# Strassen parts for the first twelve blocks of the opening group, weight sums and gating on GpSimd

## The chip, the cores and the metric

The kernel runs on one core of a Trainium2 chip. The metric is the device time of one execution in microseconds (us); lower is better. The engines are TensorE (PE in the profile; PEld are its weight loads), VectorE (DVE), ScalarE (ACT), GpSimd (POOL) and SyncE (SP), which issues most of the DMAs in the order of its queue. An engine works through its own instructions in order, and an instruction that waits holds up all that stand behind it on that engine.

## The reference

One layer of a hybrid encoder over 2048 prompt tokens and 64 sample tokens, 1024 channels, float32. Cut to what matters:

```python
h = rmsnorm(x, g1) * (1 + sc1) + sh1
u, q, k, v, o, gates = split(h @ w_in)
mix = concat([pool_mixer(u), mlstm(q, k, v, gates) * sigmoid(o)]) @ w_out
x = x + gt1 * mix                                   # attention half
h2 = rmsnorm(x, g2) * (1 + sc2) + sh2
up = h2 @ w_up                                      # 1024 -> 2 * 2816
a, g = split(b_conv + causal_conv3(up, w_conv))
x = x + gt2 * ((silu(g) * a) @ w_down)              # feed-forward half
y = rmsnorm(x, g_final)
```

## The kernel before, in words

**Precision.** Each operand of a product is split into a high and a low part (`wt[:, 0]` and `wt[:, 1]` for weights): ACT copies the value into the reduced float format, DVE subtracts to get the rest. A product then takes three passes of TensorE (`PASSES`). Weights come as a stream of units of up to 512 columns (`stream`, `issue`, `work_on`): a DMA on SP, the copy on ACT (L428), the subtraction on DVE (L431). The stream runs a few units ahead of TensorE (`pump`).

**Attention half.** Four groups of 512 tokens (the last with the 64 sample tokens as well, 576). Each group projects, runs four mLSTM heads and four pooling rows (`poolmix`, whose small copies of `u` are on POOL), and then the output projection `outproj`: eight rows of 128 output channels, each with two weight units (`w_out`, then `wo_in`), two banks of PSUM, an `x` row loaded by SP, an add on DVE (L267 by `now`), a store to `x2d` and a square on ACT that is added into `ssum`. Side work is written as generators in the lists `bg`, and the matmul loops advance them a step at a time (`tick`). One of them, `up_sums`, starts with group 1 and makes the sums of `w_up` that the feed-forward half needs: for each of 22 feature blocks and two halves it loads a tile `w4` (four buffers), does four operations on 128x256, and stores the result to `wsum`, 44 steps in all. Its instructions are pinned in program order.

At the end of the last group, after the first two output rows, `outproj` calls `leave`. It empties all these generators (`drain`), closes the storage of the attention half, opens that of the feed-forward half in its place, and starts `norm_sums`, which makes the operand sums of the opening feed-forward group: ACT issues loads of `h2d`, ACT and DVE form the tiles `hx` (L809, L795, L791).

**Feed-forward half.** Three groups of 704 tokens (`fgroups`). The up projection uses a Strassen scheme for each of the 22 feature blocks (`Pair`): seven products of operand sums (`B11`, `B21`, `T1` to `T4`, `B22`) with weights or weight sums, each 12 matmuls of 352 columns (L1616). Then the convolution (L1589, L1594), silu on ACT (L1812), gating on DVE (`Pair.gate`, L1817 and L1820), and the split of the gated rows. The blocks of a group are cut into parts (`PARTS`). A part of four blocks takes its down projection by the same scheme (`quad_down`, 168 matmuls of 352 columns, L2084), with weight sums `dsum` of `w_quad`; any other part takes the plain one (`down`, L2230: per block 8 rows x 3 passes x two column ranges of 448 and 256, so 48 matmuls). In the opening group the parts are of 6, 6, 4 and 6 blocks, only the third is a Strassen part, and `quad_sums` makes all of `dsum` on DVE as side work in that group (L1676 to L1682). In the other two groups the parts are 4, 4, 4, 4 and 6.

In the opening group three of the four weight sums of a block (`KEPT`) are split and written to `wsplit`, from which the other groups load them whole.

Of the kernel before, what the change touches and what calls it, by code (L numbers as in the profile page):

```python
# [9 lines left out]
F32 = mybir.dt.float32  # L10
F32R = mybir.dt.float32r
AF = mybir.ActivationFunctionType
ALU = mybir.AluOpType
# [53 lines left out]
def tile_layer(ctx: ExitStack, tc: tile.TileContext, xT, vecs, cst, rst, w_mod, w_ada, w_qkou, w_v, w_pool,  # L67
# [273 lines left out]

    def sum_unit(g, f, i):
# [16 lines left out]
    for g in range(NFG):  # L359
        held = None  # L360
        late = []
        for (f0, f1_) in PARTS[g]:
# [21 lines left out]
            late = []  # L384
    pend = []
# [38 lines left out]
    def work_on(u, upto):  # L424
# [5 lines left out]
        if u.state == 1 and upto > 1:  # L430
            dve.tensor_tensor(out=u.w[:, 1, :u.n], in0=u.raw[:, :u.n], in1=u.w[:, 0, :u.n].bitcast(F32), op=ALU.subtract)  # L431
            u.state = 2
# [434 lines left out]
    if True:  # L867
# [6 lines left out]
        def up_sums():  # L874

            def load(f, c):
                w = a1.tile([P, 4, 256], F32, tag="w4", name="w4", bufs=4)
                for i in range(2):
# [3 lines left out]
            todo = [(f, c) for f in range(NF) for c in (0, 256)]  # L882
# [3 lines left out]
            def store():  # L886
                if made:
                    f, c, w = made.pop()
                    pin(nc.sync.dma_start(out=wsum[f, :, :, c:c + 256], in_=w))
            yield  # L890
            yield
            for i, (f, c) in enumerate(todo):
# [9 lines left out]
                pin(dve.tensor_tensor(out=a0, in0=g1, in1=a0, op=ALU.subtract))  # L902
                pin(dve.tensor_tensor(out=a1_, in0=a1_, in1=a0, op=ALU.subtract))
# [762 lines left out]
    def quad_sums(ds):  # L1666

        for d in ds:
            for c in (0, 256):
                t = f2.tile([P, 2, FT], F32R, tag="av", name="qs", bufs=AVB)  # L1670
                w = t.bitcast(F32).rearrange("p a t -> p (a t)")[:, :1024].rearrange("p (i c) -> p i c", i=4)
                nc.sync.dma_start(out=w, in_=w_quad[d, :, :, c:c + 256])
                for _ in range(7):
                    yield
                a11, a12, a21, a22 = (w[:, i] for i in range(4))
                dve.tensor_tensor(out=a22, in0=a21, in1=a22, op=ALU.add)  # L1676
                yield
                dve.tensor_tensor(out=a21, in0=a11, in1=a21, op=ALU.subtract)
                yield
                dve.tensor_tensor(out=a11, in0=a22, in1=a11, op=ALU.subtract)  # L1680
                yield
                dve.tensor_tensor(out=a12, in0=a12, in1=a11, op=ALU.subtract)  # L1682
                yield
                yield
                nc.sync.dma_start(out=dsum[d, :, :, c:c + 256], in_=w)
                yield
                yield

# [20 lines left out]
    class Pair:  # L1709


        ended = False
# [7 lines left out]
        def products(self, old):  # L1720
# [45 lines left out]
            product(b3, Bo, "T3", False)  # L1766
            rest((older, Pair.step_7))
# [46 lines left out]
        def gate(self):  # L1814
            E = EX - 2 if self.o.last else FT
            if self.quad is None:
                dve.tensor_tensor(out=self.tg[:, :E], in0=self.ta[:, :E], in1=self.tg[:, :E], op=ALU.mult)  # L1817
                return
            for (a, b, s) in self.o.segs:
                dve.tensor_tensor(out=self.tg[:, a:b], in0=self.ta[:, a + 2 * s:b + 2 * s], in1=self.tg[:, a + 2 * s:b + 2 * s],  # L1820
# [342 lines left out]
    for o in fgroups:  # L2163
        Bo = B[o.g]
        held = None
        for pi, part in enumerate(PARTS[o.g]):
# [6 lines left out]
            if quad is not None and o.g == 0:  # L2173
                drain(0)
# [216 lines left out]
```

## Time and profile before

| | |
|---|---|
| median of three runs | 2168.68 us (2167.97 to 2169.99) |
| span of the profiled execution | 2165.8 us; no time of its own is listed beside it |
| busy: PE, PEld | 2143.9, 2038.3 us |
| busy: DVE, ACT, POOL | 1649.8, 1105.2, 265.3 us |
| HBM | 412.56 MB read, 125.98 MB written |

The profile is one execution. Its rows group instructions by line, engine and tiles: busy time, mean length in ns, and the idle time of the engine before them with what ended it. A row of a timeline begins with the start and the length in us, counted from the start of the span. A row of windows has the busy time of each engine in that stretch, with the number of instructions. Line numbers of the change below differ from those of before by some: L431 becomes L437, L898 to L903 become L908 to L913, L2084 becomes L2077, L2230 becomes L2216.

### The profile page before, as it was taken

To read this page: it belongs to the slowest core of one execution; us is meant where nothing else is said; L and a number is where in the kernel's file an instruction comes from. 1 tells how busy PE (TensorE), PEld (TensorE's weight loads), DVE (VectorE), ACT (ScalarE), POOL (GpSimd) and SP (SyncE) were. 2 spreads that over 40 slices of the span, in tenths; PEclk is the share of its full clock that TensorE was granted. 3 is DMA by queue.
4 is the path that set the end of the run, shared out by engine and by line. 5 is a ranking of instruction groups with operands and counts; after the bars stand their busy time and mean duration, and the time that the engine had idled before them with its cause. 6 is when DMAs were issued, how large, how long until landed. Compare 5 with 4: busy or idle time off the path is not lost.

```text
span 2165.8 us, 38050 instructions
## 1 busy us (share of the span) xinstructions
PE 2143.9 (99%) x13529; PEld 2038.3 (94%) x13529; DVE 1649.8 (76%) x3060; ACT 1105.2 (51%) x2193; POOL 265.3 (12%) x475
## 2 busy tenths in 40 slices
PE   8999999999999999999999999999999999999998
PEld 7888888888899999999999999999999999999998
DVE  5777679677675778788688768988877597887874
ACT  4554335234333557465556445655655365565554
POOL 0010000001000301010001220100101321111112
PEclk9999999999999999999999999999999999999999
DMA  8987997897799689797768976665668675555542
GB/s 320 331 304 225 325 311 249 292 325 259 247 294 296 207 273 317 241 343 248 229 219 305 360 282 207 228 225 202 219 234 276 221 251 190 171 175 188 172 159 76
DMA packets 297063, 541.09 MB, mean 250 GB/s; under 512 B 25728, under 2 KB 113280, under 8 KB 296872
## 3 DMA queue, kind: packets, MB, share of 16 engines
q1 hardware_dynamic: 286280, 513.44, 70.3%
q10 hardware_dynamic: 10592, 25.20, 3.0%
q8 instruction: 107, 1.75, 0.3%
q14 instruction: 84, 0.69, 0.1%
HBM read 412.56 MB, written 125.98 MB: 249 GB/s over the span
## 4 chain that ended last, share of the span: by engine, by line
PE 89%; DVE 4%; DMA 3%; issue 1%; ACT 1%; SPq 0%; POOL 0%; POOLq 0%; DVEq 0%; ACTq 0%
PE mm L1616 37%; PE mm L495 23%; PE mm L2230 11%; PE mm L2084 10%; PE mm L1155 3%; DVE wt L431 1%; PE m L1345 1%; PE m L1365 1%; PE m L1367 1%; PE m L1330 1%; DMA wt<-dsum 0%; PE mm L1091 0%; DMA qs<-w_quad 0%; DVE tg L1594 0%; DMA raw<-w_up 0%
## 5 line engine op out<-in xcount | busy, mean ns | idle before, releaser
L1616 PE MATMUL mm<-hx,wt 128*128 128x352 f32 x5544 | 886.1, 321 | 2.5 <-DVE wt L431 2.2
L1616 PEld LDWEIGHTS mm<-hx,wt 128*128 128x128 f32 x5544 | 878.3, 188 | 4.9 <-DVE wt L431 4.2
L495 PE MATMUL mm<-hl,wt 128*128 128x512 f32 (+2 forms) x1920 | 385.4, 356 | 0.0
L431 DVE TENSOR_TENSOR wt<-raw,wt 128x512 fp32r<-128x512 f32 (+1 forms) x460 | 310.8, 681 | 79.1 <-ACT wt L428 77.7
L428 ACT ACTIVATE wt<-raw 128x512 fp32r<-128x512 f32 (+1 forms) x460 | 274.7, 604 | 168.0 <-PE mm L495 53.2
L495 PEld LDWEIGHTS mm<-hl,wt 128*128 128x128 f32 x1920 | 314.7, 188 | 47.4 <-issue 4.4
L2084 PE MATMUL mm<-av,wt 128*128 128x352 f32 x1512 | 248.0, 323 | 1.7 <-DVE x L2053 0.7
L2084 PEld LDWEIGHTS mm<-av,wt 128*128 128x128 f32 x1512 | 242.3, 188 | 4.8 <-DVE ea L1625 2.8
L2230 PE MATMUL mm<-av,wt 128*128 128x448 f32 (+1 forms) x1440 | 231.4, 322 | 0.0
L2053 DVE SCALAR_TENSOR_TENSOR x<-mm,MOD,x 128x352 f32<-128x352 f32 (+3 forms) x368 | 171.9, 507 | 77.8 <-PE mm L2230 62.0
L2230 PEld LDWEIGHTS mm<-av,wt 128*128 128x128 f32 x1440 | 220.8, 188 | 9.7
L1664 ACT ACTIVATE mm<-mm 128x352 f32<-128x352 f32 x204 | 91.4, 448 | 238.9 <-PE mm L1616 175.1
L495 PE MATMUL mm<-mx,wt 128*128 128x512 f32 (+1 forms) x960 | 182.6, 352 | 0.0
L495 PEld LDWEIGHTS mm<-mx,wt 128*128 128x128 f32 x960 | 159.3, 188 | 22.5
L1594 DVE SCALAR_TENSOR_TENSOR ta<-ea,V,ta 128x704 f32<-128x704 f32 (+1 forms) x132 | 125.7, 953 | 60.4 <-ACT ta L1589 56.3
L1594 DVE SCALAR_TENSOR_TENSOR tg<-eg,V,tg 128x704 f32<-128x704 f32 (+1 forms) x132 | 125.7, 952 | 49.8 <-ACT tg L1589 47.2
L431 DVE TENSOR_TENSOR wt<-wt 128x512 fp32r<-128x512 f32 x204 | 138.7, 685 | 10.9 <-ACT wt L428 10.7
L428 ACT ACTIVATE wt<-wt 128x512 fp32r<-128x512 f32 x204 | 123.8, 622 | 25.9 <-DMA wt<-wsum 24.7
L1572 POOL COPY ea<-UC 128x2 f32<-128x2 f32 x66 | 35.0, 530 | 529.1 <-DVE ta L1594 418.4
L1812 ACT ACTIVATE tg<-tg 128x704 f32<-128x704 f32 (+1 forms) x66 | 52.5, 796 | 71.3 <-DVE tg L1594 71.3
L1155 PE MATMUL mm<-wt,hl 128*128 128x256 f32 (+1 forms) x576 | 71.2, 284 | 0.0
L1155 PEld LDWEIGHTS mm<-wt,hl 128*128 128x128 f32 x576 | 70.3, 189 | 0.8 <-issue 0.6
(305 smaller groups left out, 2222.7 us busy)
## 6 DMA issues: line engine op xcount, KB each, us to landing
wt<-wsplit SPq DMA_DIRECT2D x132, 512.0 KB, 4.2
raw<-w_up SPq DMA_DIRECT2D x198, 256.0 KB, 4.1
wt<-hl_kept SPq DMA_DIRECT2D x96, 512.0 KB, 5.9
wt<-wsum SPq DMA_DIRECT2D x132, 256.0 KB, 4.9
wsplit<-wt SPq DMA_DIRECT2D x66, 512.0 KB, 5.3
w<-w_up SPq DMA_DIRECT2D x88, 256.0 KB, 4.7
wsum<-w SPq DMA_DIRECT2D x44, 512.0 KB, 5.3
Bd<-fscr ACTq DMA_DIRECT2D x56, 352.0 KB, 3.4
```

The costliest lines, as they stand in the source:

```text
L428: act.activation(u.w[:, 0, :u.n], u.raw[:, :u.n], AF.Copy)
L431: dve.tensor_tensor(out=u.w[:, 1, :u.n], in0=u.raw[:, :u.n], in1=u.w[:, 0, :u.n].bitcast(F32), op=ALU.subtract)
L495: pe.matmul(ps[bi][:, :hi - lo], U[:, a, k % 4 * P:(k % 4 + 1) * P], mv[k][:, b, lo:hi], start=(at == 0 and pi == 0), stop=(k == order[-1] ...
L1155: pe.matmul(ps[ti][:n, :cols], h[4 * kh + k4][:, b, lo:lo + n], U[:, a, k4 % 2 * cols:(k4 % 2 + 1) * cols], start=(kh == 0 and k4 == 0 and ...
L1572: pool.tensor_copy(ext[:, 0:2], UC[:, f, :])
L1594: dve.scalar_tensor_tensor(out=t[:, :E], in0=ext[:, j:j + E], scalar=wc(j, f), in1=t[:, :E], op0=ALU.mult, op1=ALU.add)
L1616: pe.matmul(bk.t[:, :FH], U[:, a, kc * P:(kc + 1) * P], Bo.at(nm, kc, b), start=(first and kc == 0 and pi == 0), stop=(kc == 3 and pi == 2 ...
L1664: act.activation(to.t[:, :FH], bk.t[:, :FH], AF.Copy)
L1812: act.activation(self.tg[:, :E], self.tg[:, :E], AF.Silu)
L2053: dve.scalar_tensor_tensor(out=x3[n][:, a:b], in0=bk.t[:, a - lo:b - lo], scalar=gt2(n, s), in1=x3[n][:, a:b], op0=ALU.mult, op1=ALU.add)
L2084: pe.matmul(bk.t[:, :FH], U[:, a, c:c + P], quad.put(op, m, b), start=(first and m == 0 and pi == 0), stop=(m == 1 and pi == 2), skip_grou ...
L2230: pe.matmul(bks[i].t[:, :hi - lo], U[:, a, k % 4 * P:(k % 4 + 1) * P], av[k][:, b, lo:hi], start=(k == 0 and (a, b) == PASSES[0]), stop=(k ...
```

## The change

Four things change. In the opening group the first twelve blocks are cut into three Strassen parts of four, so that its parts become those of the other groups. The sums of `w_quad` for all Strassen parts (`dsum`) leave that group: `quad_sums` is removed, and its 16 steps stand behind the 44 of `up_sums`, which does its operations on POOL in place of DVE. The gating of the opening group is done by POOL and is called one product earlier than the next block's steps. And for one of the three kept weight sums (`WS4`) the low half is made by POOL in that group.

```diff
-PARTS = (((0, 6), (6, 12), (12, 16), (16, 22)), ((0, 4), (4, 8), (8, 12), (12, 16), (16, 22)),
+PARTS = (((0, 4), (4, 8), (8, 12), (12, 16), (16, 22)), ((0, 4), (4, 8), (8, 12), (12, 16), (16, 22)),
          ((0, 4), (4, 8), (8, 12), (12, 16), (16, 22)))
-SUMS = ((6, 7, 0, 1, 2), (3, 4, 5))
...
+        if i == WS4 and g == 0:
+            fourth.append(kept)
...
+    aside = {i for i, u in enumerate(stream) if u[-1] is not None and len(u) == 4 and u[2] == INSIDE and
+             any(u[3] is k for k in fourth)}
...
-            dve.tensor_tensor(out=u.w[:, 1, :u.n], in0=u.raw[:, :u.n], in1=u.w[:, 0, :u.n].bitcast(F32), op=ALU.subtract)
+            e = pool if u.at in aside else dve
+            e.tensor_tensor(out=u.w[:, 1, :u.n], in0=u.raw[:, :u.n], in1=u.w[:, 0, :u.n].bitcast(F32), op=ALU.subtract)
...
                 w = a1.tile([P, 4, 256], F32, tag="w4", name="w4", bufs=4)
+                if f >= NF:
+                    tc.keep_in_program_order(nc.sync.dma_start(out=w, in_=w_quad[f - NF, :, :, c:c + 256]))
+                    return w
...
-            todo = [(f, c) for f in range(NF) for c in (0, 256)]
+            todo = [(f, c) for f in range(NF + 2 * QUADS) for c in (0, 256)]
...
-                    pin(nc.sync.dma_start(out=wsum[f, :, :, c:c + 256], in_=w))
+                    to = wsum[f] if f < NF else dsum[f - NF]
+                    pin(nc.sync.dma_start(out=to[:, :, c:c + 256], in_=w))
...
-                pin(dve.tensor_tensor(out=g1, in0=g0, in1=g1, op=ALU.add))
-                pin(dve.tensor_tensor(out=g0, in0=a0, in1=g0, op=ALU.subtract))
+                pin(pool.tensor_tensor(out=g1, in0=g0, in1=g1, op=ALU.add))
+                pin(pool.tensor_tensor(out=g0, in0=a0, in1=g0, op=ALU.subtract))
...
-                pin(dve.tensor_tensor(out=a0, in0=g1, in1=a0, op=ALU.subtract))
-                pin(dve.tensor_tensor(out=a1_, in0=a1_, in1=a0, op=ALU.subtract))
+                pin(pool.tensor_tensor(out=a0, in0=g1, in1=a0, op=ALU.subtract))
+                pin(pool.tensor_tensor(out=a1_, in0=a1_, in1=a0, op=ALU.subtract))
...
-    def quad_sums(ds):
...
             product(b3, Bo, "T3", False)
+            if o.g == 0:
+                rest((old, Pair.gate))
             rest((older, Pair.step_7))
...
         def gate(self):
             E = EX - 2 if self.o.last else FT
+            if self.multiplied:
+                return
+            self.multiplied = True
+            e = dve if self.o.g else pool
             if self.quad is None:
-                dve.tensor_tensor(out=self.tg[:, :E], in0=self.ta[:, :E], in1=self.tg[:, :E], op=ALU.mult)
+                e.tensor_tensor(out=self.tg[:, :E], in0=self.ta[:, :E], in1=self.tg[:, :E], op=ALU.mult)
                 return
...
-            if quad is not None and o.g == 0:
-                drain(0)
-                aside, bg[1][:] = list(bg[1]), []
...
-                    bg[0].append(quad_sums(SUMS[0]))
                     bg[1].append(prepare(fgroups[1], fscr))
...
-                    if o.g == 0:
-                        bg[0].append(quad_sums(SUMS[1]))
-                        bg[1].extend(aside)
```

Where the instructions stand now, at three places. First the queue of SP at the end of the attention half, from the store of `o_pool` on. Before, it holds the x rows (`scr`), the weights of the output projection and the stores of its rows:

```order
L1458 DMA o_pool<-PO 128x120
L608 DMA scr<-xT 128x576
L407 DMA raw<-w_out 128x512
L407 DMA raw<-wo_in 128x512
L407 DMA raw<-w_out 128x512
L407 DMA raw<-wo_in 128x512
L661 DMA x2d<-scr 128x576
```

After the change, the same place (`w_7815` and so on are buffers of `w4`, each with one step's sums):

```order
L1468 DMA o_pool<-PO 128x120
L614 DMA scr<-xT 128x576
L899 DMA dsum<-w_7815 512x1x256
L885 DMA w_8199<-w_quad 128x4x256
L899 DMA dsum<-w_8001 512x1x256
L885 DMA w_8206<-w_quad 128x4x256
...
L899 DMA dsum<-w_8283 512x1x256
L667 DMA x2d<-scr 128x576 x2
L614 DMA scr<-xT 128x576
L667 DMA x2d<-scr 128x576
L412 DMA raw<-wo_in 128x512
```

All 16 stores to `dsum` stand in one run with 13 loads, ahead of the store of the first two output rows, the x of row 3 and five weight units of the output projection; before, x rows and weights follow one another.

Second, ACT at the same place. Before, the loads of `h2d` and the first high halves of the operand sums (`hx`) stand ahead of the square into `ssum`:

```order
L829 DMA fscr<-h2d 128x704 x4
L428 ACTIVATE wt<-raw 128x512
L809 ACTIVATE hx<-fscr 128x352 x4
L428 ACTIVATE wt<-raw 128x512
L522 ACTIVATE ssum<-scr 128x576
```

After:

```order
L433 ACTIVATE wt<-raw 128x512 x4
L531 ACTIVATE scr<-scr 128x576
L528 ACTIVATE ssum<-scr 128x576
L835 DMA fscr<-h2d 128x704 x4
L815 ACTIVATE hx<-fscr 128x352 x2
L433 ACTIVATE wt<-raw 128x512
```

The square has moved ahead of the loads. In the program it waits for POOL and for eight DMA queues, where before it waited for one queue and DVE.

Third, POOL from the end of the sums into the opening feed-forward group. Before, it holds only the small copies of the convolution there; after:

```order
L913 TENSOR_TENSOR w_8283<-w_8283 128x256
L1565 MEMSET UC 128x88
L437 TENSOR_TENSOR wt<-wt 128x512
L1582 COPY ea<-UC 128x2
...
L1582 COPY eg<-UC 128x2
L1596 COPY UC<-ea 128x2
L437 TENSOR_TENSOR wt<-wt 128x512
L1596 COPY UC<-eg 128x2
L1582 COPY ea<-UC 128x2
L1813 TENSOR_TENSOR tg<-ta,tg 128x704
```

The low halves (L437) and the gating (L1813, and L1810 in the plain part) stand between the copies. Over the whole program PE has 864 plain down matmuls (1440 before) and 2016 half products (1512 before). DVE has 240 operations of the sums fewer; POOL has 240 more of 128x256, 22 more of 128x512 and 22 more for the gating.

More of the change, by code (lines that the diff above doesn't have):

```diff
@@ L340, in tile_layer @@
     wsplit = dr.tile([NF, len(KEPT), P, 2, 512], F32, tag="wsplit", name="wsplit")
+    fourth = []
     def sum_unit(g, f, i):
@@ L1664, in seed @@
         act.activation(to.t[:, :FH], bk.t[:, :FH], AF.Copy)
-    def quad_sums(ds):
[L1668 to L1687, printed above, removed]
     def half_tile(nm):
@@ L1709, in tile_layer @@
     class Pair:
-        ended = False
+        ended = multiplied = False
         quad = d = None
```

2 lines of the change are left out of this document (1 added, 1 removed).

## The prediction

> **What bounds the kernel now.** I read the page first, then the windows by stage, then the timeline of the end of the attention half, engine by engine.
>
> ```profile
> span 2165.8 us, 38050 instructions
> PE 2143.9 (99%) x13529; PEld 2038.3 (94%) x13529; DVE 1649.8 (76%) x3060; ACT 1105.2 (51%) x2193; POOL 265.3 (12%) x475
> 240.00:737.00 497.00, 496.24 (x3014) 438.10 (x3013) 363.74 (x795) 193.66 (x497) 42.74 (x53) 1.00 0.85 280
> 737.00:787.00 50.00, 50.00 (x377) 50.00 (x377) 42.53 (x92) 26.55 (x53) 3.10 (x6) 1.00 0.78 262
> 787.00:1249.00 462.00, 460.30 (x2893) 452.67 (x2893) 366.29 (x602) 263.79 (x474) 58.43 (x95) 1.00 0.83 283
> ```
>
> The columns after the length are PE, PEld, DVE, ACT, POOL, granted clock, DMA share. TensorE is busy for 496.24 of 497 us while the attention groups 1 to 3 run, for all 50 us of the last output projection, and for 460.30 of 462 us in the opening feed-forward group. So the time is the TensorE work, and there are two ways to move it: fewer matmuls, or a hole. Three runs gave 2167.97 to 2169.99 us; their median 2168.68 stands 2.9 us over the profiled span of 2165.8, and I add the changes of the span to the median. Some 0.2% (4 us) is what a measurement of this kernel can tell from no change.
>
> **Part 1, fewer matmuls.** Group 0 gets three more Strassen parts in place of two plain ones. The order of instructions has 576 fewer plain down matmuls and 504 more half products, 72 fewer in all.
>
> ```profile
> L1616 PE MATMUL mm<-hx,wt 128*128 128x352 f32 x5544 | 886.1, 321 | 2.5 <-DVE wt L431 2.2
> L2084 PE MATMUL mm<-av,wt 128*128 128x352 f32 x1512 | 248.0, 323 | 1.7 <-DVE x L2053 0.7
> L2230 PE MATMUL mm<-av,wt 128*128 128x448 f32 (+1 forms) x1440 | 231.4, 322 | 0.0
> ```
>
> Busy time over count gives 164.0 ns for a half product and 160.7 ns for a plain one: 504 x 0.164 - 576 x 0.1607 = -9.9 us. With one price for both (886.1 / 5544 = 159.8 ns) it is -11.5 us. I take **-11**.
>
> **Part 2, the sums.** The generator that makes the weight sums goes from 44 steps to 60, because the 16 steps for the down weights join its end, and its arithmetic goes from DVE to POOL.
>
> ```profile
> L902 DVE TENSOR_TENSOR w<-w x44: 408/424/428, 240.8 to 736.3; 128x256 f32<-128x256 f32 x44
> 738.93 0.80 POOL L1427 COPY PO<-u 128x15 f32<-128x15 f32 x1
> L2033 POOL TENSOR_TENSOR y<-x,fscr 128x256 f32<-128x256 f32 x2 | 1.4, 726 | 2.0 <-ACT fscr L2001 2.0
> ```
>
> Its pace is set by the matmuls that advance it, and the 44 steps already last from 240.8 to 736.3 us, to the end of the half. The other 16 have no place there. `leave` empties the generator in one go, after the first two output rows, and the order has them so: on POOL 64 operations directly after the last copy (739.7 us in before), on SP a run of 16 stores and 13 loads. A 128x256 operation of two tensors takes POOL 726 ns where nothing disturbs it. So the run lasts at least 64 x 0.726 = 46.5 us, and its last store is issued no sooner than 786. In a sentence by itself: the Trainium skill (GPSIMD Engine Reference, section Performance versus the Vector engine) counts about 2.6 cycles of 1.2 GHz per element of a two-input operation, by which I would estimate 0.56 us for one, 36 us for the run, and a total about 11 us below mine; the row has 0.726, and the row decides.
>
> The transfers can make it longer. With four buffers the load of step k+4 waits until the store of step k has landed:
>
> ```profile
> L1672 SPq DMA_DIRECT2D qs<-w_quad x16: 547/642/1607, 815.0 to 1204.0; - x16
> DMA to landing us min/median/max: 3.7/6.7/8.5
> L1685 SPq DMA_DIRECT2D dsum<-qs x16: 519/523/629, 840.5 to 1238.9; - x16
> DMA to landing us min/median/max: 3.4/5.6/8.3
> ```
>
> The same load and store take 6.7 and 5.6 us in the median, so four steps take 5.6 + 6.7 + 2.9 = 15.2 us, 3.8 each; with the shortest landings POOL's 2.9 stays the limit. From a first store at 742.6 the last is issued 15 steps later, between 786 and 800. I take 793.
>
> What is queued behind it: on SP the x of output row 3 and the weights from the second half of row 5 on. On ACT the square into `ssum`, whose tile lies in the storage that the sums release, and which now waits for POOL and eight DMA queues; behind that, ACT's loads of h2d for the operand sums of the feed-forward half. On DVE the add of row 3, and after it all these operand sums. TensorE has rows 2, 3 and 4 before it needs any of this.
>
> ```profile
> 786.96 2.08 PE L1616 MATMUL mm<-hx,wt 128*128 128x352 f32 x12
> 772.61 0.33 SPq L661 DMA_DIRECT2D x2d<-scr  x1
> 779.08 0.33 SPq L661 DMA_DIRECT2D x2d<-scr  x1
> 742.19 2.22 ACTq L829 DMA_DIRECT2D fscr<-h2d  x4
> 747.39 0.50 ACT L809 ACTIVATE hx<-fscr 128x352 fp32r<-128x352 f32 x1 [2.24 <-DMA fscr<-h2d]
> 751.33 0.67 ACT L522 ACTIVATE ssum<-scr 128x576 f32<-128x576 f32 x1
> 767.00:787.00 20.00, 20.00 (x152) 20.00 (x152) 19.27 (x43) 11.25 (x23) 0.00 (x0) 1.00 0.82 274
> ```
>
> The feed-forward half starts at 786.96 now, and a row lasts 6.47 us (779.08 - 772.61), so TensorE stands from about 786.96 - 3 x 6.47 = 767.6. The restart: last store issued 793; landed 5.6 later; the square 0.67; from the issue of the h2d loads to the first operand 5.2 (747.39 - 742.19); then the DVE work up to the last operand of the first product. Between the add of row 3 and that operand the order has 58 DVE instructions, of the kinds that DVE does now at 767 to 787: 19.27 / 43 = 0.448 us each, 26 us. To these I add 3.5 us for the waits on the h2d loads of the second half, which come in pairs behind the DVE. Sum: 793 + 5.6 + 0.7 + 5.2 + 26 + 3.5 = 834, against 787: **+47**. The three rows that TensorE still has (2.5 x 6.47 = 16 us) fit beside it. Ends: 786 + 3.4 + 0.7 + 5.2 + 26 = 821 (+34), and 800 + 8.3 + 0.7 + 5.2 + 26 + 10 = 850 (+63). By itself: the Trainium skill (TensorE: Matmul & The Clock Gate, Part 1) halves the clock for about 3.4 us after an idle window, an estimate of 1.7 us for each restart; it is not in the sum, and the only thing like it in before is the clock of 0.94 in the last 54 us, where TensorE has gaps:
>
> ```profile
> 2112.00:2166.00 54.00, 45.78 (x297) 43.45 (x295) 25.67 (x58) 22.04 (x41) 14.48 (x15) 0.94 0.22 77
> ```
>
> **Part 3, POOL beside DVE in the attention half.** 176 DVE operations of 0.42 us go (74 us), 176 of 0.726 come to POOL. TensorE can't gain from the relief, since it idles only 0.76 us there. It can lose: POOL's small copies for the pooling rows stand behind sums.
>
> ```profile
> 722.96 8.33 POOL L1426 COPY PO<-u 128x15 f32<-128x15 f32 x1 [1.20 <-ACT u L267]
> 1228.13 1.71 POOL L2045 TENSOR_TENSOR ssum<-ssum,fscr 128x704 f32<-128x704 f32 x1 [2.39 <-ACT fscr L2044]
> 1228.54 1.84 DVE L431 TENSOR_TENSOR wt<-raw,wt 128x512 fp32r<-128x512 f32 x1 [1.05 <-ACT wt L428]
> L431 DVE TENSOR_TENSOR wt<-wt 128x512 fp32r<-128x512 f32 x204 | 138.7, 685 | 10.9 <-ACT wt L428 10.7
> ```
>
> The two engines keep each other out: a copy of 15 elements lasted 8.33 us while DVE ran without a gap, and a DVE operation of 0.685 us lasted 1.84 because POOL had begun 0.4 us earlier. Once at the end of each of three groups such a wait may show: 0 to 3 x 8.3 = 25 us, and since one engine's gap lets the other in, I stay near the low end: **+4**. Below nothing only by the 0.76.
>
> **Part 4, the opening feed-forward group.** DVE loses 64 sums (0.42), 22 gatings and 22 low halves (0.685). It gains 40 adds of rows, 42 operations on half tiles, and 26 more wide and 16 fewer narrow weight halves.
>
> ```profile
> L1817 DVE TENSOR_TENSOR tg<-ta,tg 128x704 f32<-128x704 f32 x24 | 21.2, 884 | 2.1 <-ACT tg L1812 2.1
> L2053 DVE SCALAR_TENSOR_TENSOR x<-mm,MOD,x 128x352 f32<-128x352 f32 x152 | 84.3, 579 | 11.0 <-PE mm L2084 10.6
> L1828 DVE TENSOR_TENSOR av<-tg,av 128x352 fp32r<-128x352 f32 x54 | 28.2, 522 | 12.1 <-ACT av L1825 12.1
> ```
>
> Out: 27 + 22 x 0.884 + 22 x 0.685 = 61 us. In: 40 x 0.579 + 42 x 0.522 + 26 x 0.685 - 16 x 0.42 = 56 us. So DVE keeps 366 - 5 = 361 us in a group of 451. POOL gets 22 x 1.71 for the gating and 22 x about 1.28 for the low halves (between 0.726 for 256 columns and 1.71 for 704): 66 us. Even if no operation of one ran beside the other, 361 + 66 = 427 us fit into 451. Locally it costs: the gating's reader is queued on ACT and DVE one product later, and a held DVE operation loses 1.84 - 0.685 = 1.16 us. Ends: 0, if DVE's idle 90 us take it all, and 44 x 1.16 = 51 us, if nothing hides it. I take **+5**, nearer to nothing, because the Strassen part there now runs at the full rate with DVE at a similar load. Edits at nothing: 24 more bank copies on ACT (264 of 462 us busy hide them), and the new DMAs of w_quad and dsum, against which the sums' own traffic leaves this group.
>
> **Sum.** 2168.7 - 11 + 47 + 4 + 5 = **2214 us**.
>
> **The rivals.**
> - *The restart is cheap* (chance 0.12): the wait of `ssum` is met before the last store has landed, and the operand sums run during the block, so only the weights of rows 5 to 7 hold TensorE: 786 + 5 for landing and splitting + 16 = 807, a hole of 20 us. 2168.7 - 11 + 20 + 9 = 2187. For it: the order gives waits, not when they are met. Against it: DVE's add of row 3 stands ahead of the operand sums, and its x is behind the block on SP.
> - *DVE and POOL lock in group 0* (0.15): half of the 1.16 us per POOL operation is not hidden, 20 us more than I took: 2234. The Trainium skill (SBUF — State Buffer, section Who interferes with whom) speaks against the change here: a DVE instruction with two SBUF inputs and a reading GpSimd instruction block each other fully, and whoever comes second waits for the end. The pair at 1228 us agrees. It decides if TensorE's waits on `wt` and `av` sum to over 10 us in that group.
> - *Faster* (0.05): the 16 steps are over before TensorE runs dry. With 37 us of restart behind the last store, the hole is under 11 us only if the block ends by 761, so if a POOL operation took (761 - 739.7) / 64 = 0.33 us or less. It then takes 2168.7 - 11 + 4 = 2162. Against it: 726 ns in the row, and 0.42 even on DVE.
>
> **How the numbers follow.** My forecast has 0.68; 2214 is its value, with 2192 (the hole at 34, nothing in parts 3 and 4) to 2238 (the hole at 63, and 8 more of part 4) as its bounds. The first rival lies at 2187 and the second at 2234, so a range of 2185 to 2238 leaves out the faster case and the tails. Faster by over 0.2%: 0.05. Within 0.2%: 0.02, for a block that ends near 772. Slower: 0.93.
>
> **What would show it.** Right: a gap of TensorE between the output projection and the first up product in two pieces, 40 to 60 us in all, granted clock under 1.00 around it; 16 stores to dsum on SP in a row, about 3 us apart, with no weight load between them; ACT waiting before the square into `ssum`; plain down matmuls x864, half products x2016. Wrong: dsum stores spread over the attention half, weight loads or operand sums going on between them, or POOL's 128x256 operation far from 0.73 us; and, for part 4, TensorE below 445 busy us in the 451 of group 0.

## The result, and the profile after

The changed kernel takes 2244.4 us (median of four runs, 2244.2 to 2245.82) against 2169.34 us of the kernel before on the same chip (2167.97 to 2173.0): a ratio of 1.0345, 95% interval 1.0331 to 1.036. The prediction was 2214 us with a range of 2185 to 2238: the direction was right, and 30 us were missing.

The profiled execution has a span of 2242.6 us, 76.8 more than before. The first lines of its page:

```profile
span 2242.6 us, 38158 instructions
PE 2154.9 (96%) x13457; PEld 2046.1 (91%) x13457; DVE 1669.3 (74%) x2868; ACT 1128.4 (50%) x2245; POOL 555.2 (25%) x759
```

Its windows, in the columns of those shown of before:

```profile
240.00:737.00 497.00, 485.87 (x2898) 426.44 (x2897) 330.10 (x598) 182.60 (x476) 189.09 (x210) 0.99 0.83 279
751.22:866.77 115.55, 70.97 (x466) 69.31 (x465) 53.80 (x105) 33.51 (x68) 54.81 (x71) 0.81 0.85 278
866.77:1331.44 464.67, 450.49 (x2775) 442.84 (x2775) 398.00 (x577) 285.46 (x519) 133.92 (x139) 0.99 0.76 253
```

TensorE has 72 matmuls fewer, as the order said, and loses time in three places. During the attention groups it now idles for 11 of 497 us (0.76 before). From the last output projection to the first up products (second row) it idles for 44.6 us, 36.12 of them in one piece. And in the opening feed-forward group it is busy for 450.49 of 464.67 us.

To share the 76.8 us out, four events on TensorE cut the span: the first matmul of the last output projection that reads `mx`, and the matmuls over `ssum` that stand early in each of the three feed-forward groups. In TensorE's timeline after, these four, and second and third among the rows the ones behind the long gap and at the last operand of the first up product (start, length, and in brackets the wait with what ended it):

```profile
751.22 4.01 PE L501 MATMUL mm<-mx,wt 128*128 128x256 f32 x29
819.50 9.13 PE L501 MATMUL mm<-mx,wt 128*128 128x256 f32 x48 [36.12 <-DVE scr L266]
854.44 0.59 PE L1626 MATMUL mm<-hx,wt 128*128 128x352 f32 x2 [3.39 <-DVE hx L801]
866.77 0.39 PE L541 MATMUL m<-ones_r,ssum 128*128 128x1 f32 x3
1331.44 0.72 PE L1928 MATMUL m<-ones_r,ssum 128*128 128x1 f32 x6
1783.29 0.95 PE L1928 MATMUL m<-ones_r,ssum 128*128 128x1 f32 x8
```

The four events in TensorE's timeline before:

```profile
735.76 1.50 PE L495 MATMUL mm<-mx,wt 128*128 128x256 f32 x10
799.48 0.72 PE L535 MATMUL m<-ones_r,ssum 128*128 128x1 f32 x6
1254.10 1.06 PE L1935 MATMUL m<-ones_r,ssum 128*128 128x1 f32 x9
1707.32 0.83 PE L1935 MATMUL m<-ones_r,ssum 128*128 128x1 f32 x7
```

| stage (differences of these starts) | before, us | after, us | change | predicted |
|---|---|---|---|---|
| attention half, up to the last output projection | 735.76 | 751.22 | +15.5 | +4 |
| restart: last output projection and first up products | 63.72 | 115.55 | +51.8 | +47 |
| opening feed-forward group | 454.62 | 464.67 | +10.1 | -11 + 5 |
| next group | 453.22 | 451.85 | -1.4 | 0 |
| the rest | 458.48 | 459.31 | +0.8 | 0 |

**The attention half.** DVE's timeline after, ahead of the first large wait of TensorE in these groups:

```profile
276.94 1.21 DVE L224 SCALAR_TENSOR_TENSOR acc<-raw,CA,acc 128x512 f32<-128x512 f32 x1
278.07 1.22 DVE L224 SCALAR_TENSOR_TENSOR s<-raw,CA,s 128x512 f32<-128x512 f32 x1
...
281.47 0.74 DVE L224 SCALAR_TENSOR_TENSOR s<-raw,CA,s 128x512 f32<-128x512 f32 x1
282.14 0.74 DVE L224 SCALAR_TENSOR_TENSOR acc<-raw,CA,acc 128x512 f32<-128x512 f32 x1
282.80 0.68 DVE L266 TENSOR_TENSOR kw<-m,CL 128x512 f32<-128x512 f32 x1
```

POOL's beside it, where the last row is its last operation before 284 us:

```profile
277.68 1.06 POOL L909 TENSOR_TENSOR w<-w 128x256 f32<-128x256 f32 x1
278.82 1.06 POOL L912 TENSOR_TENSOR w<-w 128x256 f32<-128x256 f32 x1
279.95 1.05 POOL L913 TENSOR_TENSOR w<-w 128x256 f32<-128x256 f32 x1
```

And TensorE's:

```profile
283.53 2.09 PE L1355 MATMUL m<-va,kw 128*128 128x129 f32 x8 [4.02 <-DVE kw L266]
285.27 4.91 PE L501 MATMUL mm<-hl,wt 128*128 128x512 f32 x12
```

DVE and POOL take turns. While POOL works, DVE starts an operation every 1.14 us (276.94, 278.07) and POOL one in the same 1.14 (277.68, 278.82); once POOL has stopped, DVE starts one every 0.67 (281.47, 282.14). So one POOL operation takes some 0.47 us from a DVE with a full queue, and the same sum takes DVE only 0.42 us when DVE does it. The move relieved nothing there, and `kw` (a tile of an mLSTM head that DVE makes) came late behind that queue. TensorE's waits in the attention groups after are 8.3 us on `kw` in two gaps and 2.9 us on `va`, `mx` and `scr`; before, they were 0.8 in all. Behind such a gap TensorE is also slower: the 12 matmuls of 512 columns took 3.02 us here in the kernel before, and now 4.91.

**The restart.** This is the stage with the hole of the prediction. SP's timeline after, from the first of the 16 stores to the last:

```profile
761.09 0.56 SPq L899 DMA_DIRECT2D dsum<-w  x1
...
805.23 7.18 SPq L899 DMA_DIRECT2D dsum<-w  x3
812.46 1.61 SPq L667 DMA_DIRECT2D x2d<-scr  x2
814.12 0.73 SPq L614 DMA_DIRECT2D scr<-xT  x1
```

And ACT's behind it:

```profile
815.28 0.69 ACT L528 ACTIVATE ssum<-scr 128x576 f32<-128x576 f32 x1 [48.80 <-DMA dsum<-w]
815.29 3.80 ACTq L835 DMA_DIRECT2D fscr<-h2d  x4
```

The 16 stores stand in one block of 51 us, and ACT waits 48.80 us before the square into `ssum`, until the last one has landed. DVE stands for the same square:

```profile
816.00 0.76 DVE L532 TENSOR_TENSOR ssum<-ssum,scr 128x576 f32<-128x576 f32 x1 [44.45 <-ACT ssum L528]
```

Its add of output row 3, for which TensorE waits in the long gap, comes only behind this, at 818.87 us, when the `x` row issued at 814.12 has landed. So two things hold row 3: the release of the storage, through this wait of DVE, and the queue of SP. Of the 51.8 us by which this stage is longer, 44.6 are idle time of TensorE. The other 7.2 are the same work done more slowly: it is busy for 70.97 us with a granted clock of 0.81, where before it needed 63.72 at 1.00.

**The opening feed-forward group.** Its three kinds of matmul in that stretch before: up products, half products, plain ones (length of the stretch, then TensorE's busy time and count):

```profile
799.48:1254.10 454.62, 288.21 (x1802) 284.91 (x1800) 1.00 0.83 283
799.48:1254.10 454.62, 27.41 (x168) 26.94 (x168) 1.00 0.83 283
799.48:1254.10 454.62, 138.51 (x864) 132.35 (x864) 1.00 0.83 283
```

After:

```profile
866.77:1331.44 464.67, 293.83 (x1801) 289.44 (x1800) 0.99 0.76 253
866.77:1331.44 464.67, 111.82 (x672) 108.10 (x672) 0.99 0.76 253
866.77:1331.44 464.67, 46.18 (x288) 44.14 (x288) 0.99 0.76 253
```

The down products fell from 165.9 to 158.0 us, 7.9 less. The same up products take 5.6 us more. TensorE's idle time in this stretch rose from 1.7 us (454.62 less 452.92 busy) to 14.2, 12.5 more. The three make the +10. The granted clock has a part in it. In two places of this group it fell to 0.50 for about 3.4 us, behind waits of only 1.86 us (to 1081.06) and 1.43 us (to 1186.72):

```profile
1081.00:1085.00 4.00, 3.94 (x15) 3.94 (x16) 4.00 (x6) 2.71 (x5) 2.35 (x2) 0.57 0.64 205
1187.00:1191.00 4.00, 4.00 (x17) 4.00 (x17) 4.00 (x8) 0.78 (x2) 0.51 (x1) 0.57 0.75 255
```

Each costs 1.7 us (0.43 of the four). By where the up products stand in TensorE's timeline I estimate that 2.8 of these 3.4 us fall on them.

### The profile page after: what moved, and what is told of

It reads as the page before. It is cut to its first block, busy times and chain, and to the rows that moved or that the text cites. A ratio compares the mean times of both kernels' runs of the same rounds, so it can differ in the third digit from the quotient of the medians.

```text
span 2242.6 us, 38158 instructions
## 1 busy us (share of the span) xinstructions
PE 2154.9 (96%) x13457; PEld 2046.1 (91%) x13457; DVE 1669.3 (74%) x2868; ACT 1128.4 (50%) x2245; POOL 555.2 (25%) x759
## 4 chain that ended last, share of the span: by engine, by line
PE 72%; DVE 11%; DMA 7%; issue 5%; POOL 3%; ACT 2%; SPq 1%; DVEq 0%; POOLq 0%; ACTq 0%
PE mm L1626 30%; PE mm L501 15%; PE mm L2077 12%; PE mm L2216 6%; PE mm L1165 3%; DVE wt L437 3%; DVE tg L1604 1%; DMA scr<-xT 1%; DVE scr L266 1%; PE m L1355 1%; ACT tg L1599 1%; DMA raw<-w_up 1%; DMA wt<-wsum 1%; DMA hl_kept<-wt 1%; POOL w L908 1%
## 5 line engine op out<-in xcount | busy, mean ns | idle before, releaser
L437 DVE TENSOR_TENSOR wt<-raw,wt 128x512 fp32r<-128x512 f32 (+2 forms) x446 | 320.4, 724 | 74.5 <-ACT wt L433 73.0
L2077 PE MATMUL mm<-av,wt 128*128 128x352 f32 x2016 | 332.4, 324 | 8.1 <-DVE ea L1635 5.5
L433 ACT ACTIVATE wt<-raw 128x512 fp32r<-128x512 f32 (+2 forms) x446 | 269.4, 611 | 127.6 <-PE mm L501 32.7
L2046 DVE SCALAR_TENSOR_TENSOR x<-mm,MOD,x 128x352 f32<-128x352 f32 (+5 forms) x408 | 193.8, 517 | 55.7 <-PE mm L2216 38.3
L501 PE MATMUL mm<-mx,wt 128*128 128x512 f32 (+2 forms) x960 | 189.6, 361 | 41.3 <-DVE scr L266 36.9
L437 DVE TENSOR_TENSOR wt<-wt 128x512 fp32r<-128x512 f32 x206 | 153.4, 745 | 2.9 <-ACT wt L433 2.8
L433 ACT ACTIVATE wt<-wt 128x512 fp32r<-128x512 f32 x228 | 139.3, 623 | 24.6 <-DMA wt<-wsum 17.1
L2216 PE MATMUL mm<-av,wt 128*128 128x448 f32 (+1 forms) x864 | 139.1, 322 | 0.0
L437 POOL TENSOR_TENSOR wt<-wt 128x512 fp32r<-128x512 f32 x22 | 32.5, 1476 | 199.4 <-ACT wt L433 177.7
L908 POOL TENSOR_TENSOR w<-w 128x256 f32<-128x256 f32 x60 | 55.0, 916 | 99.0 <-DMA w<-w_up 96.6
```

The lines of the kernel that those rows point to most:

```text
L433: act.activation(u.w[:, 0, :u.n], u.raw[:, :u.n], AF.Copy)
L501: pe.matmul(ps[bi][:, :hi - lo], U[:, a, k % 4 * P:(k % 4 + 1) * P], mv[k][:, b, lo:hi], start=(at == 0 and pi == 0), stop=(k == order[-1] ...
L908: pin(pool.tensor_tensor(out=g1, in0=g0, in1=g1, op=ALU.add))
L2046: dve.scalar_tensor_tensor(out=x3[n][:, a:b], in0=bk.t[:, a - lo:b - lo], scalar=gt2(n, s), in1=x3[n][:, a:b], op0=ALU.mult, op1=ALU.add)
L2077: pe.matmul(bk.t[:, :FH], U[:, a, c:c + P], quad.put(op, m, b), start=(first and m == 0 and pi == 0), stop=(m == 1 and pi == 2), skip_grou ...
L2216: pe.matmul(bks[i].t[:, :hi - lo], U[:, a, k % 4 * P:(k % 4 + 1) * P], av[k][:, b, lo:hi], start=(k == 0 and (a, b) == PASSES[0]), stop=(k ...
```

## The experiments

The table has each run's changes of a stage against the kernel before, cut at the same four events of its profile. Five runs whose programs are the same up to the last output projection (but for the engine that issues the first loads of `w_quad` in poolq) reach it at 750.74 to 751.87 us, so a difference of some 1 us there means nothing; in the opening group, runs with the same work in it differ by up to 2 us.

| run | median us | ratio, 95% interval | attention half | restart | opening group |
|---|---|---|---|---|---|
| changed kernel | 2244.4 | 1.0345, 1.0331 to 1.036 | +15.5 | +51.8 | +10.1 |
| paced | 2203.96 | 1.0152, 1.0137 to 1.0167 | +20.8 | +6.1 | +10.3 |
| sums_dve | 2226.08 | 1.0257, 1.0241 to 1.0272 | +0.4 | +49.0 | +10.3 |
| pool44 | 2187.29 | 1.0076, 1.0059 to 1.0093 | +15.7 | +3.2 | +1.0 |
| poolq | 2306.28 | one run | +15.1 | +114.8 | +8.9 |
| g0_dve | 2237.81 | 1.0312, 1.0296 to 1.0327 | +16.0 | +52.2 | +3.4 |
| gate_dve | 2235.06 | 1.0302, 1.0287 to 1.0318 | +15.0 | +50.5 | +0.7 |
| ws4_dve | 2242.23 | 1.0343, 1.0329 to 1.0357 | +16.1 | +53.6 | +8.6 |
| strassen_dve | 2184.47 | 1.0072, 1.0057 to 1.0087 | +7.7 | +6.9 | +1.5 |
| strassen_dve_late_gate | 2185.16 | 1.0072, 1.0055 to 1.0089 | +7.2 | +9.3 | +1.7 |
| transfers | 2175.74 | 1.0029, 1.0018 to 1.004 | +6.5 | 0.0 | +2.1 |
| early | 2207.26 | 1.0179, 1.0165 to 1.0193 | +35.0 | +7.0 | +0.6 |
| before_ws4 | 2169.95 | 1.0007, 0.9999 to 1.0016 | -1.0 | 0.0 | +2.1 |

### paced: the 16 steps out of the closing

```diff
                 w = nx.pop(0)
                 yield
-                yield
```

> The changed kernel with one pause fewer in each step of the sums (three instead of four), so that all 60 steps have been issued, among the other work, before the attention half is closed and nothing is left to empty there. Theory (the hole comes from emptying 16 steps in one run): the gap of TensorE between the output projection and the first up product goes to 5 us or less, the end of that stage comes 52 us sooner; the POOL operations beside the attention groups grow from 44 to 60 steps, so what they cost there grows from 15.5 to about 21 us; span 2242.6 - 52 + 6 = 2197 us. Rival (POOL is too slow for 60 steps wherever they stand, and the closing waits for it all the same): POOL runs late, over 25 us of the hole stay, span 2220 us or more.

Span 2201.6 us. The restart costs 6.1 us in place of 51.8; TensorE's longest wait at that place is 3.45 us. The attention half went to +20.8, with 60 POOL steps in it in place of 44. The gap and the attention half are those of the first theory, which had 5 us or less and about +21; the 6.1 us that the restart keeps it did not have. The rival, by which over 25 us of the hole stay, falls.

### sums_dve: is it POOL's rate?

```diff
-                pin(pool.tensor_tensor(out=g1, in0=g0, in1=g1, op=ALU.add))
+                pin(dve.tensor_tensor(out=g1, in0=g0, in1=g1, op=ALU.add))
...
```

> The changed kernel with the arithmetic of all 60 steps back on DVE; the 16 steps are still emptied in one run. If POOL's rate sets the length of the run: a step takes 4 x 0.42 = 1.7 us, the run 27 us instead of 51, the hole about 28 us. If the transfers of load and store set it (four buffers, 5.6 + 6.7 + 1.7 us round, 3.5 us a step): the run stays near 50 us and the hole at 45 us or more. In both cases the 15.5 us of the attention groups go away if they come from POOL beside DVE. Span 2203 us by the first, 2220 us or more by the second; if the attention loss does not come from POOL, 15 us more in each.

Span 2224.0 us, the second answer. The first and the last of the 16 stores in its SP timeline:

```profile
744.06 0.56 SPq L899 DMA_DIRECT2D dsum<-w  x1
...
794.72 0.51 SPq L899 DMA_DIRECT2D dsum<-w  x1
```

And DVE's waits from 744 to 800 us (us in total, times, longest):

```profile
DVE w L908 <- DMA w<-w_quad: 17.6, 10, 2.4
```

The block lasts the same 51 us with an operation that is almost twice as fast, because DVE now waits for the loads. That the four buffers hold the loads back is argued from the order; no run has more of them. On POOL it is its own rate that sets the length: it waits for loads for only 2.4 us in the whole block and starts an operation every 0.80 us, and 64 of these are 51 us. So two limits of the same size meet here. The attention half is back at +0.4, so its loss is POOL's.

### pool44: POOL beside DVE in the attention half, alone

In the kernel before:

```diff
-                pin(dve.tensor_tensor(out=g1, in0=g0, in1=g1, op=ALU.add))
+                pin(pool.tensor_tensor(out=g1, in0=g0, in1=g1, op=ALU.add))
...
```

> The kernel before with one edit: the arithmetic of the 44 steps of the sums on POOL. Theory (DVE and POOL keep each other out, TensorE then waits for DVE's small tiles in the attention groups): the attention half ends 15 us later, span 2165.8 + 15 = 2181 us, and nothing else moves. Rival (the prediction's +4; the rest of the loss seen in the changed kernel belongs to something else there): span 2170 us.

Span 2185.1 us. The attention half loses 15.7 us, as in the changed kernel, and TensorE waits 4.02 and 4.27 us for `kw` at the same two places. My +4 falls. The restart loses 3.2 us more, which the expectation did not have and no run explains.

### poolq: the queue of SP or the release of the storage?

```diff
-                    tc.keep_in_program_order(nc.sync.dma_start(out=w, in_=w_quad[f - NF, :, :, c:c + 256]))
+                    tc.keep_in_program_order(nc.gpsimd.dma_start(out=w, in_=w_quad[f - NF, :, :, c:c + 256]))
...
-                    pin(nc.sync.dma_start(out=to[:, :, c:c + 256], in_=w))
+                    pin((nc.sync if f < NF else nc.gpsimd).dma_start(out=to[:, :, c:c + 256], in_=w))
```

> The changed kernel, where the loads of w_quad and the stores to dsum are issued by POOL in place of SP. The 16 steps are still emptied in one run, and the square into the tile ssum still waits for their storage, but the x rows and the weights of the output projection no longer stand behind them on SP. If the blocked queue makes the whole hole: hole 10 us or less, span 2200 us or less. If the release of the storage makes it by itself: the last store is still issued at about 812 us, the square comes at about 816, the operand sums after it; TensorE can run all eight rows (to about 803) and then waits for about 20 to 37 us, span 2212 to 2228 us. The prediction's first rival said that freeing the x rows and weights would leave 20 us or less.

The numbers of both theories were off, because a queue that does arithmetic, store and load in turn needs some 8 us a step in place of 3.4; the last store is issued at 884.59. But the question is answered all the more plainly. TensorE's timeline around the hole:

```profile
789.74 6.54 PE L501 MATMUL mm<-mx,wt 128*128 128x320 f32 x49
891.71 1.47 PE L1626 MATMUL mm<-hx,wt 128*128 128x352 f32 x3 [95.43 <-ACT hx L815]
```

And ACT's at its end:

```profile
888.09 0.68 ACT L528 ACTIVATE ssum<-scr 128x576 f32<-128x576 f32 x1 [93.48 <-DMA dsum<-w]
```

With x rows and weights free, TensorE gets through most of the output projection, to 796.3 us. Then it stands for 95 us, because the square into `ssum` still waits for the last store, and the operand sums stand behind it. So the release of the storage is enough for a hole, in the one execution there is. The blocked queue adds to it: from the square to the matmul over `ssum` it is 51.5 us in the changed kernel (815.28 to 866.77) and 41.3 here (888.09 to 929.43), where fewer rows are left to do.

### g0_dve, gate_dve, ws4_dve: POOL in the opening group

```diff
-            e = dve if self.o.g else pool
+            e = dve
```

```diff
-            e = pool if u.at in aside else dve
+            e = dve
```

gate_dve has the first edit, ws4_dve the second, g0_dve both.

> The changed kernel with the gating and the low half of WS4 in the opening feed-forward group back on DVE. Theory (POOL beside DVE costs the group some 16 us more than I took): the group comes out 10 to 21 us shorter, span 2222 to 2232 us. Rival (the three Strassen parts in themselves load DVE and the weight stream too much; DVE then has to do 35 us more): the group stays or grows, span 2242 us or more. Attention half and hole as in the changed kernel under both.

> The changed kernel with only the gating back on DVE; the low half of WS4 stays on POOL. Both back gave 6.6 us in the opening feed-forward group (464.7 to 458.1). If the loss goes with POOL's busy time beside DVE (22 operations of each kind, 40 us of gating, 32 us of low halves): the group at 461, span 2239 us. If the late low half (TensorE waits on wt) is what costs: the group stays at 464, span 2242 us. If the gating alone costs: 458, span 2236 us.

> The changed kernel with only the low half of WS4 back on DVE; the gating stays on POOL. The runs so far have the opening feed-forward group at 464.7 us with both on POOL, 458.1 with both on DVE, 455.4 with only the low half on POOL. If the two add: 464.7 + 2.7 = 467.4 us in the group, span 2245 us. If gating on POOL hurts only together with the low half on POOL: 460 us or less, span 2238 us or less.

The group takes 464.67 us with both on POOL, 463.20 with the gating alone on POOL, 455.36 with the low half alone, 458.05 with neither. The gating costs 5 to 9 us. The low half comes out at 1.5 worse or 2.7 better, and at 0.8 better against strassen_dve (456.11), whose group is the same as that of g0_dve. Runs with the same group differ by up to 2 us, so no gain or loss can be told. DVE's own weight halves in the changed kernel, by groups in that stretch:

```profile
L437 DVE TENSOR_TENSOR wt<-raw,wt 128x512 fp32r<-128x512 f32 (+1 forms) x104 | 82.1, 795 | 10.3 <-ACT wt L433 10.3
L437 DVE TENSOR_TENSOR wt<-wt 128x512 fp32r<-128x512 f32 x94 | 76.4, 812 | 1.6 <-ACT wt L433 1.6
```

And in gate_dve:

```profile
L437 DVE TENSOR_TENSOR wt<-raw,wt 128x512 fp32r<-128x512 f32 (+1 forms) x104 | 72.4, 702 | 7.6 <-ACT wt L433 7.6
L437 DVE TENSOR_TENSOR wt<-wt 128x512 fp32r<-128x512 f32 x94 | 64.3, 684 | 0.1
```

With the gating on POOL these 198 operations take 21.8 us longer. DVE was to be relieved of 22 gatings of 0.884, 19.4 us. It pays more than that in its other work. What is not explained by POOL stays too: with the gating on DVE the group is +0.6 to +3.4 in six runs, not at -11.

### strassen_dve and strassen_dve_late_gate: the Strassen parts alone

strassen_dve joins the edits of paced, sums_dve and g0_dve. The other run also takes out:

```diff
-            if o.g == 0:
-                rest((old, Pair.gate))
```

> The Strassen parts alone: the changed kernel with the sums on DVE, their 60 steps paced as in the run with one pause fewer, and gating and the low half of WS4 on DVE. If the three parts of the loss only add: attention half +0 to 1 us, restart +3 to 6, opening feed-forward group +3.4, next group -1.4; span 2165.8 + 5 to 9 = 2171 to 2175 us, still not faster than before. If the prediction's price for the fewer matmuls holds once nothing disturbs them (-11): span 2160 us or less.

> The run of the Strassen parts alone, with the gating of the opening group at its old place, after the next block's first product. If the early place makes DVE late for the convolution's tiles (TensorE waits on ea and wt): the group gets 2 to 5 us shorter, span 2167 to 2171 us. If the place does nothing: span within 1 us of the run with the early gating. If the early place helps: longer.

Spans 2181.3 and 2183.5 us. The early place of the gating does nothing. Restart and group came out near the sum (+6.9 for +3 to 6, +1.5 for +3.4), but the attention half did not: 60 steps in it cost 7.7 us on DVE too. The -11 is not to be had: in the opening group of strassen_dve the down products take 157.0 us (8.9 less than before) and the up products 292.1 (3.9 more), and the idle time is 8.5 us (6.8 more).

### transfers: is it DVE's work or the DMAs?

In strassen_dve:

```diff
+                if f < NF:
-                pin(dve.tensor_tensor(out=g1, in0=g0, in1=g1, op=ALU.add))
+                    pin(dve.tensor_tensor(out=g1, in0=g0, in1=g1, op=ALU.add))
...
```

> The run of the Strassen parts alone, but the 16 steps for dsum only load and store: their 64 DVE operations are left out, so dsum holds copies of w_quad and the down products of the Strassen parts are wrong by that. The run of the Strassen parts alone lost 7.7 us in the attention half and 6.9 us from there to the end of the restart. If DVE's 64 more operations (27 us) make these: the attention half back to +0 to 1, the restart to +0 to 2, span 2167 to 2170 us. If the 16 more loads and stores (DMA share 0.92 in place of 0.85) make them: both stay, span 2180 us or more. Between: the split tells the shares.

The added sums are left out, so `dsum` holds the weights as they were loaded. Span 2173.6 us, between the two, and the split is clean. The attention half stays at +6.5: DVE's 64 operations don't make it. What is left for it is the 16 loads and stores and the closer pace of the steps, which no run parts. The restart falls to 0.0: its 6.9 us were DVE's 64 operations. The windows of the attention groups, first of this run, with the same DMA share of 0.92 that strassen_dve has and 0.85 before:

```profile
240.00:737.00 497.00, 491.35 (x2958) 430.16 (x2957) 357.11 (x785) 189.01 (x487) 41.79 (x47) 1.00 0.92 311
```

And of strassen_dve:

```profile
240.00:737.00 497.00, 491.53 (x2957) 430.32 (x2956) 375.77 (x841) 187.79 (x486) 41.38 (x47) 1.00 0.92 310
```

TensorE gets equally far in both, though DVE has 18.7 us less to do in the first, and less than in the kernel before (363.74). In both TensorE waits for loads of `hl_kept`, 1.8 and 2.0 us, which it never does in these groups before.

### early: begin the sums a group sooner

The edits of sums_dve and gate_dve (the low half stays on POOL), the old pace, and:

```diff
-            if o.g == 1:
-                bg[4].append(up_sums())
...
                 bg[3].append(ada(2, True))
+                bg[4].append(up_sums())
```

> The changed kernel put right as far as the runs point: the sums on DVE at their old pace, but begun in the first attention group in place of the second, so that all 60 steps are issued before the attention half is closed; the gating on DVE; the low half of WS4 still on POOL. If the 7.7 us that 60 paced steps on DVE cost in the attention half came of their density (DVE and transfers in groups 1 to 3): attention half +0 to 3 us, restart +3, opening feed-forward group +0.7, next group -1.4; span 2168 to 2171 us, a tie with before. If it is the work itself, wherever it stands: attention half +8, span 2175 us. If the prediction's -11 is still to be had: 2158 us.

A miss: span 2206.4 us. From 240 us on the attention groups run as before (494.09 of 495 us busy), but the first group lost 35 us. The window from 40 to 212 us here:

```profile
40.00:212.00 172.00, 149.48 (x757) 120.91 (x757) 116.31 (x248) 74.10 (x175) 9.52 (x14) 0.94 0.87 296
```

And in the kernel before:

```profile
40.00:212.00 172.00, 169.89 (x912) 143.85 (x911) 131.83 (x249) 93.99 (x205) 10.65 (x14) 1.00 0.81 281
```

There the transfers were already at 0.81 and TensorE's waits are on weights (8.5 us on ACT's `wt`), on `nd` (5.8) and on an `xT` load (5.6). That the transfers delay them is likely, but no run took them apart there.

### before_ws4: the one part that looked like a gain

In the kernel before, the low half of `WS4` on POOL in the opening group, as in the change.

> The kernel before with one edit: the low half of WS4 in the opening feed-forward group on POOL, the one part of the change that came out as a gain (2.7 us in that group, where DVE had 383 us of work in 458). Here DVE has 361 us and TensorE waits for only 1.7 us in that group. If it can only take TensorE's waits away: span 2164 to 2166 us, a tie. If POOL beside DVE costs as elsewhere: 2168 us or more. If DVE's load slows TensorE without showing as waits: 2162 us or less.

A tie, 1.0007 (0.9999 to 1.0016), with the group 2.1 us longer. The gain of 2.7 us in gate_dve is no gain elsewhere. None of the runs beats the kernel before.

## Why the prediction was wrong in size

In spans, 45 us were forecast and 76.8 came. Of the 31.8 us between them, 16.1 are in the opening group (parts 1 and 4), 11.5 in the attention half (part 3) and 4.8 in the hole (part 2); the stages behind take back 0.5. The mechanism of the hole was right. That of parts 3 and 4, that POOL's work beside DVE is nearly free, was not.

**The hole: right, in place and in mechanism.** I had the first store at 742.6 and the last at 793; they came at 761.09 and 811.9, with the 50 us between them as predicted, and 18.5 later, of which the attention half had lost 15.5. The length is partly luck: I took a middle between POOL's busy time of 0.726 an operation and a round of transfers of 3.8 us a step, and what set it was a term I didn't have, the 0.80 us from start to start. Landing took 3.4 us, not 5.6; from the square to the last operand of the first up product (854.44) it took 39.2, where I had 35.4. The hole is 51.8 against 47. I had looked for 40 to 60 us of gaps in two pieces; there are 44.6, one of 36.12 and several of at most 3.39. The clock's part, which I kept out of the sum at 1.7 us for each restart, is 7.2 us, more than the 4.8 that were missing. paced shows that the emptied run causes the hole, sums_dve that it is as long with DVE adding, and poolq that the release of `ssum`'s storage is enough for one. That is the end of the rival of a cheap restart: it asked that the wait of `ssum` be met early.

**Part 3, +4: a step that failed.** It measured +15.5, and pool44 shows it alone. The step was "TensorE can't gain from the relief ... I stay near the low end, since one engine's gap lets the other in". I looked for the cost in POOL's small copies at the end of each group. It was in the middle of the groups, where DVE has a queue without gaps and POOL has one too. I had the row for it: a DVE operation of 0.685 us that lasted 1.84 beside POOL. I used it in the feed-forward group and not here, though DVE is busy for 364 of 497 us here as well. The Trainium skill (SBUF — State Buffer, section Who interferes with whom) names this pair, a DVE instruction with two inputs in SBUF and a GpSimd instruction that reads there, as one that contends for a port pair, and calls that pair an exclusive lock. The trace agrees in kind and not in full: a pair takes 1.14 us, less than 0.67 and POOL's undisturbed 0.80 from start to start together.

Of the 15.5 us, 10.4 are waits (11.2 less the 0.8 of before). Most of the rest fits the clock behind the two long gaps (1.9 us on the 12 matmuls above alone). The windows of the changed kernel behind the first:

```profile
283.50:285.00 1.50, 1.47 (x7) 1.47 (x8) 1.40 (x3) 0.00 (x0) 0.00 (x0) 0.50 1.07 398
285.00:286.90 1.90, 1.90 (x7) 1.61 (x7) 1.81 (x5) 0.63 (x1) 0.00 (x0) 0.50 1.08 391
286.90:288.90 2.00, 2.00 (x7) 1.52 (x6) 1.90 (x4) 0.00 (x0) 0.00 (x0) 0.50 1.06 394
```

A wait of 4.02 us was followed by 5.4 us at 0.50. The Trainium skill (TensorE: Matmul & The Clock Gate, Part 1) puts the clock at half after an idle window of about 3.4 us, and the trace agrees here. But the waits of 1.86 and 1.43 us in the opening group were followed by half the clock too, so in this kernel that figure is no bound below which a wait costs only itself.

**Part 4, +5: a step that failed.** TensorE is busy for 450.49 of 464.67 us, 97%, where I had put the line at 445 of 451, which is 98.7%; measured as a share, part 4 was wrong by its own test. The second rival, by which the two engines hold each other up, is half right. It asked for waits of over 10 us on `wt` and `av`; there are 7.2 on `wt`, none on `av`, and 5.5 on `ea`. Its mechanism is in the gating (5 to 9 us), but not in the low half, which costs or gains nothing that can be told. My "427 us fit into 451" failed twice. It took DVE's 361 us as given, and DVE is busy for 398.00 us: its other operations get longer beside POOL by more than the gating took away. And it left out the copies that POOL already made in that stretch, 58.43 us in the row that I had shown. With them the same sum is 485 and doesn't fit, though part of these copies' time is itself waiting for DVE.

**Part 1, -11: the price was near, the sum was not reached.** The fewer matmuls are worth 7.9 to 8.9 us by the down products. What I had at nothing took it back. The up products cost 3.9 us more in strassen_dve, with the clock at 1.00 throughout, and 5.6 in the changed kernel, of which some 2.8 are the clock. TensorE's idle time grew by 6.8 us even with nothing on POOL, most of it in waits on DVE's `wt` and `ea`. DVE had no more to do than I had counted: with gating and low halves back on it, 34.5 us by my prices, strassen_dve should have it busy for 395 us, and it has 383 of 456. Why the up products got dearer at an undisturbed clock stays open, and so does why DVE came late with that load.

Together: +15.5 for +4, +51.8 for +47 and +10.1 for -6 are 32.4 us more, and with -1.4 and +0.8 behind the group 31.8, which makes 76.8 of 45.

## What to carry to other kernels

Before work goes to a second engine that takes turns with the first, look at what the first does at the same time: where its queue is full, 0.42 us of relief cost 0.47. A generator that the matmuls advance has a capacity, and steps past it don't disappear; they are emptied where the storage closes, in series, with the next stage waiting for the release. And side work brings its transfers along: 16 loads and 16 stores of 512 KB in a stage whose DMAs are at 0.85 cost 6.5 us with the closer pace that they asked for, of the 8 to 9 that the fewer matmuls gave.

## What the runs showed of the hardware

- POOL and DVE in turns: 128x256 on POOL and 128x512 on DVE, each with two inputs, make a pair every 1.14 us; alone POOL takes 0.73 us (0.80 from start to start) and DVE 0.67.
- Under a DVE without gaps a POOL copy of 15 elements took 8.49 us in paced, as the 8.33 of before; undisturbed it took 0.19 to 0.20.
- Loads and stores issued by POOL itself, between its operations, made a step of 8 us out of one of 3.4.
- After waits of 1.86 and 1.43 us in the changed kernel, and of 1.86 in paced and in sums_dve, TensorE's granted clock was 0.50 for about 3.4 us. After one of 1.70 us in strassen_dve_late_gate it stayed at 1.00.
